# The last MLP of a two-layer decoder trunk in two phases: its first product by seven block products, the hidden layer through DRAM, then its second product

## The chip, the cores and the metric

The kernel runs on one core of a Trainium2 chip. The metric is the device time of one execution in microseconds. The kernel before was run three times: 2396.58, 2397.88 and 2399.75 us, median 2397.88 us. TensorE is called PE below, VectorE DVE, ScalarE ACT, GpSimd POOL and SyncE SP, as in the profile. "MM" is one matmul instruction.

## The reference, cut to what matters

Two decoder layers over 1024 tokens of width 1024, all in float32. Layer 0 mixes tokens with an mLSTM, layer 1 with latent attention on a shared K/V. After each mixer stands an MLP with a hidden width of 4096. The change touches the MLP of layer 1 alone, and of that only the second half of the tokens.

```python
D_MODEL, SEQ, DEPTH, D_FF = 1024, 1024, 2, 4 * 1024

def sqrelu_mlp(h, w1, w2):
    return jnp.square(jax.nn.relu(h @ w1)) @ w2

for l in range(DEPTH):
    ...                                            # mixer: y
    x = x + g1[:, None, :] * rmsnorm(y, norm_g[l, 1])
    h = modulate(rmsnorm(x, norm_g[l, 2]), sh2, sc2)
    y = sqrelu_mlp(h, mlp_w1[l], mlp_w2[l])
    x = x + g2[:, None, :] * rmsnorm(y, norm_g[l, 3])
```

## The kernel before, in words

**Numbers.** Each float32 product is made of three PE products. Both operands are split into a high part (the value rounded to the PE's fp32r format) and a low part (the rest). `mm3` (L230 to L233) issues low times high, high times low, high times high into one PSUM tile. The high part of a weight tile is an ACT cast (L189), the low part a DVE subtraction (L190); both are in `wsplit`.

**Tokens.** They are worked in two halves of 512. `hfs[0]` and `hfs[1]` hold what belongs to a half. Normalized activations lie with the model width on the partitions and 512 tokens along the row.

**The MLP** (`mlp`) has two kinds of steps. A hidden step (L947) takes 128 columns of the first matrix, makes 8 x 3 = 24 MMs of 128x512 into a `ps` tile, and then ReLU (L957), square (L958) and the split into `hd` (L470, L471). An up step (`up_rows`, L973) multiplies four hidden blocks by a 512-column block of the second matrix, 24 MMs of 128x512 into a `pm` tile, and a DVE addition (L198) sums the result into `y`. For the last half the call is `mlp(1, hfs[1], u1, [4] * 8, True)`: four hidden steps, then hidden and up steps alternate, and at the end up steps alone. Hidden values never leave SBUF.

**Buffers.** PSUM: `ps` has 2 buffers of one bank, `pc` 2 of one bank, `pm` 2 of two banks. SBUF: `k4` 24 tiles of 128x1024, `hd` 8, `ws` 8 (the split weights), `raw` 4 (where weights land by DMA), `tmc` 6 and `tmp` 3 of 128x512.

**Order.** The program is written as generators. `go` takes one step of the dense stream (the MLP) and ties what is issued to the last PE instruction so far, so PE runs in the order of the code. A scheduler orders the other engines by priority; what stands in a `high_priority` block comes earlier. Each engine then runs its list in order, and SP issues the DMAs in order. Before the last MLP `two_streams` runs the MLP of half 0 beside the mixer of half 1 (`mixer1`), whose last part, `post`, makes the normalized input of the last MLP.

**The fill.** Beside the last MLP runs the generator `all_out`, advanced by one after each of its steps: `x_to_rows(0)` (16 advances; eight sets of four PE transposes, L1572, ACT copies and DMAs), `along_rows` (L1586 to L1590), `rows_out` of half 0 (L1593 on: for each of four row tiles two ACT squares with a sum, L1606, whose result goes unread into a `ps` tile, then DVE work L1611 to L1616 and the output DMA), and `x_to_rows(1)`. `rows_out` of half 1 comes after the last MM.

Of the kernel before, what the change touches and what calls it, by code (L numbers as in the profile page):

```python
# [17 lines left out]
P = 128  # L18
# [64 lines left out]
def kernel(  # L83
# [39 lines left out]
    def k4v(dt=F32, b=512):  # L123
        return k4(dt)[:, :1024].rearrange("p (a b) -> p a b", b=b)
# [7 lines left out]
    def raw(dt=F32):  # L132
        return sb.tile([P, 1024], dt, tag="raw", bufs=RAW, name=f"raw_{next(uid)}")
# [13 lines left out]
    def ps():  # L147
        return pp.tile([P, 512], F32, tag="ps", bufs=2, name=f"ps_{next(uid)}")
# [10 lines left out]
    def scratch(shape, name):  # L159
        return dr.tile(shape, F32, tag=name, bufs=1, name=name)  # L160
# [21 lines left out]
    def paced():  # L182

        return tc.issue_after(pace[0]) if pace[0] else nullcontext()

    def wsplit(r, n):
        hi = sb.tile([P, 1024], F32R, tag="ws", bufs=WS, name=f"wh_{next(uid)}")
        lo = sb.tile([P, 1024], F32R, tag="ws", bufs=WS, name=f"wl_{next(uid)}")
        nc.scalar.copy(hi[:, :n], r[:, :n])  # L189
        i = nc.vector.tensor_sub(lo[:, :n], r[:, :n], hi[:, :n].bitcast(F32))  # L190
        if follow[0]:
            pace[0] = i.ins
        return hi, lo
# [31 lines left out]
    def wcols(w, c0, n=P, k0=0, nk=KD):  # L225
        return w[k0 * P : (k0 + nk) * P, c0 : c0 + n].rearrange("(k p) n -> p k n", p=P)

    pe_last = [None]

    def mm3(o, lh, ll, rh, rl, start, stop):  # L230
        nc.tensor.matmul(o, ll, rh, start=start, stop=False)  # L231
        nc.tensor.matmul(o, lh, rl, start=False, stop=False)  # L232
        pe_last[0] = nc.tensor.matmul(o, lh, rh, start=False, stop=stop)  # L233


    nc.scalar.preload_act_table_set("natural_log_exp_and_others")
# [239 lines left out]
    def normed(h, xs_, rstd, A, sh):  # L476

        for k in range(KD):
            with paced():
                nc.vector.scalar_tensor_tensor(  # L480
                    xs_[k], xs_[k], A[:, k : k + 1], rstd, ALU.mult, ALU.mult
                )
                split_mod(h.hi[k], h.lo[k], xs_[k], sh[:, k : k + 1])
            if k % 4 == 3:
                yield 1

    def along_tokens(dst, y):
# [450 lines left out]
    NF = DFF // P  # L938
    AHEAD = 2

    def mlp(l, hf, y, sizes, rows=False):


        w1, w2, h = mlp_w1[l], mlp_w2[l], hf.h2
        hids = {}

        def hidden(f):  # L947
# [24 lines left out]

        def up_rows(fs, i, last):  # L973


            G = len(fs)
            if G == 2:
                g, t0, t1 = i, 0, 4
            else:
                g, t0 = (i % 2, i // 2 * 2) if last else (i // 2, i % 2 * 2)  # L980
                t1 = t0 + 2
            key = (fs[0], g)
            final = last and G == 4 and i
# [12 lines left out]
            def block(pt, ws, t):  # L996
                for q, f in enumerate(fs):
                    w, (hh, hl) = ws[q // 2], hids[f]
                    mm3(
                        pt, hh[:, ts(t, P)], hl[:, ts(t, P)], w[0][:, q % 2], w[1][:, q % 2],  # L1000
                        q == 0, q == G - 1,
                    )

            def one(ws):


                for n, (t, h) in enumerate([(0, 1), (1, 1)] if i == 1 else [(i, 0), (i, 1)]):
                    if n:
                        yield "within"
                    pt = pc()  # L1010
                    block(pt, ws if i == 1 else ws[h], t)
                    accumulate((t, h), y.t[t][:, h], pt)

            def out(ws):
                for t in range(t0, t1):
                    if t % 2 == 0:
                        if t > t0:
                            yield "within"
                        b2 = pm()
                    block(b2[:, t % 2], ws, t)  # L1020
                    if t % 2:
                        for e in range(2):
                            accumulate((t - 1 + e, g), y.t[t - 1 + e][:, g], b2[:, e])

            return load, one if final else out

        def up_cols(fs, i, last):
            G = len(fs)
            n = KD // G

            def out(w):
# [12 lines left out]
            return lambda: wload([(0, 0, wcols(w2, i * n * P, n * P, fs[0], G))], n * P), out  # L1044

        up = up_rows if rows else up_cols
        steps, prev, f0 = [], [], 0
# [10 lines left out]
        ready = []  # L1058
        for n in range(len(steps) + AHEAD):
            if n < len(steps):  # L1060
                ready.append(steps[n][0]())
            if n >= AHEAD:
                yield from steps[n - AHEAD][1](ready.pop(0))

                yield steps[(n - AHEAD + 1) % len(steps)][1].__name__


    rope_d = scratch([2, P, S], "rope_d")
# [679 lines left out]
    A1 = gain(2, NG(0, 2), adac(0, SC2))  # L1748
    B1 = gate(3, NG(0, 3), adac(0, G2))

    def post(hf, y, B, src, A, sh):
# [5 lines left out]
        yield 0  # L1757
        hf.h2 = Split()
        yield from normed(hf.h2, y, rstd, A, sh)

# [126 lines left out]
    rope_perm()  # L1887


    z1 = FH(claim=True)  # L1890
    ya = [None, None]

    def mixer1(hf, z, attention):
        att = attention(hf)
        lat = latent(hf, lambda: next(att))
        next(lat)

        yield from to_x(hf, z)
        yield "fill"
        yield from lat  # L1900
        yield next(att)
        yield from att
# [6 lines left out]
        yield from post(hf, y, B2, x_cols, A3, adac(1, SH2))  # L1909
# [6 lines left out]
    u1 = FH(claim=True)  # L1916

    def all_out():
        yield from x_to_rows(0)
# [43 lines left out]
```

## Time and profile before

| what | value |
|---|---|
| median of three runs | 2397.88 us |
| span of the profiled execution | 2395.7 us |
| PE busy | 2364.8 us |
| DVE busy | 1550.3 us |
| ACT busy | 1054.9 us |
| moved by DMA | 374.48 MB, mean 156 GB/s |
| first hidden step of the last MLP | 2027.41 us |
| last MM starts | 2386.78 us |

All times of the trace count from the start of the span. The profiled execution's own time is its span, 2395.7 us; the median of the runs is 2.2 us above it. PE is busy for all but some 31 us of the span; a group's line gives busy time, the mean of one instruction in ns, and the idle time of the engine just before it. The start of an MM to the start of the next is its pace, and is shorter than its duration, because MMs are pipelined.

### The profile page before, as it was taken

How to read it: one execution, taken by the hardware profiler on the slowest of the kernel's cores; microseconds unless marked ns; L12 is line 12 of the kernel's file. 1: busy time of each engine (PE TensorE's matmuls, PEld its weight loads, DVE VectorE, ACT ScalarE, POOL GpSimd, SP SyncE). 2: the span in 40 equal slices, each digit the busy share in tenths (PEclk: the TensorE clock that was granted, in tenths of full speed). 3: DMA queues.
4: the chain of work that ended last, by engine and by line, in shares of the span. 5: the costliest groups of instructions: out<-in, count | busy, mean ns of one | idle time of the engine just before them, and what ended most of it. 6: DMA issues, size and time to landing. Idle time of an engine off the chain costs nothing.

```text
span 2395.7 us, 30518 instructions
## 1 busy us (share of the span) xinstructions
PE 2364.8 (99%) x11621; PEld 1945.5 (81%) x11621; DVE 1550.3 (65%) x2431; ACT 1054.9 (44%) x1712; POOL 18.3 (1%) x91
## 2 busy tenths in 40 slices
PE   7999999999999999999999999999999999999998
PEld 5888888788888887888888877888888888888886
DVE  6667866858656677877764867766566386353345
ACT  4355334655333454444444554344444353443333
POOL 1000000000000000000000000000000000000000
PEclk9999999999999999999999999999999999999999
DMA  8442654544654745545543444864424354354431
GB/s 310 148 143 81 192 178 134 165 132 150 189 171 152 243 138 179 159 160 186 168 137 114 153 162 153 260 240 133 139 97 150 105 167 128 101 189 140 144 99 62
DMA packets 377106, 374.48 MB, mean 156 GB/s; under 512 B 24355, under 2 KB 282464, under 8 KB 376960
## 3 DMA queue, kind: packets, MB, share of 16 engines
q1 hardware_dynamic: 376672, 372.44, 48.9%
q8 instruction: 91, 1.49, 0.3%
q14 instruction: 55, 0.45, 0.1%
q0 software_dynamic: 288, 0.10, 0.0%
HBM read 313.24 MB, written 59.24 MB: 155 GB/s over the span
## 4 chain that ended last, share of the span: by engine, by line
PE 91%; DVE 4%; DMA 3%; ACT 1%; issue 1%; SPq 0%; DVEq 0%; ACTq 0%
PE ps L231 17%; PE ps L232 17%; PE ps L233 17%; PE pm L231 10%; PE pm L232 10%; PE pm L233 10%; PE pc L1445 1%; PE pc L231 1%; PE pc L233 1%; PE pc L232 1%; PE pm L815 1%; PE pm L1331 1%; DMA raw<-in_mlp_w_dram 1%; DVE wl L190 1%; PE pm L1325 1%
## 5 line engine op out<-in xcount | busy, mean ns | idle before, releaser
L190 DVE TENSOR_TENSOR wl<-raw,wh 128x1024 fp32r<-128x1024 f32 (+2 forms) x366 | 438.7, 1202 | 449.5 <-ACT wh L189 442.3
L189 ACT CAST wh<-raw 128x1024 fp32r<-128x1024 f32 (+2 forms) x366 | 376.0, 1032 | 717.0 <-PE ps L231 392.2
L231 PE MATMUL ps<-k,wl 128*128 128x512 f32 x1528 | 611.0, 400 | 2.3 <-ACT k L671 1.4
L233 PE MATMUL ps<-k,wh 128*128 128x512 f32 x1528 | 601.0, 393 | 0.0
L232 PE MATMUL ps<-k,wh 128*128 128x512 f32 x1528 | 600.9, 393 | 0.0
L231 PEld LDWEIGHTS ps<-k,wl 128*128 128x128 f32 x1528 | 287.0, 188 | 69.7 <-issue 2.9
L233 PEld LDWEIGHTS ps<-k,wh 128*128 128x128 f32 x1528 | 287.0, 188 | 67.3 <-issue 0.5
L232 PEld LDWEIGHTS ps<-k,wh 128*128 128x128 f32 x1528 | 287.5, 188 | 63.6 <-issue 1.7
L198 DVE TENSOR_TENSOR k<-k,pm 128x512 f32<-128x512 f32 (+1 forms) x254 | 210.9, 859 | 107.0 <-PE pm L233 106.5
L231 PE MATMUL pm<-hd,wl 128*128 128x512 f32 x512 | 202.0, 394 | 0.4 <-ACT hd L470 0.4
L233 PE MATMUL pm<-hd,wh 128*128 128x512 f32 x512 | 199.8, 391 | 0.0
L232 PE MATMUL pm<-hd,wh 128*128 128x512 f32 x512 | 199.5, 390 | 0.2 <-DVE hd L471 0.2
L231 PE MATMUL pm<-wh,hd 128*128 128x512 f32 x488 | 192.9, 395 | 3.2 <-ACT raw L1337 2.9
L232 PE MATMUL pm<-wl,hd 128*128 128x512 f32 x488 | 191.3, 392 | 0.0
L233 PE MATMUL pm<-wh,hd 128*128 128x512 f32 x488 | 190.3, 390 | 0.0
L360 DVE SCALAR_TENSOR_TENSOR tma<-raw,cond,tma 128x512 f32<-128x512 f32 x168 | 125.6, 747 | 20.6 <-DMA raw<-in_kv_ada_w_dram 14.6
L471 DVE TENSOR_TENSOR hd<-tmp,hd 128x512 fp32r<-128x512 f32 x128 | 88.3, 690 | 56.8 <-ACT hd L470 56.5
L1337 ACT ACTIVATE raw<-pm,sm 128x128 f32<-128x128 f32 (+3 forms) x64 | 47.5, 742 | 151.3 <-DVE sm L1336 122.7
L232 PEld LDWEIGHTS pm<-hd,wh 128*128 128x128 f32 x512 | 96.2, 188 | 21.3 <-DVE hd L471 0.5
L231 PEld LDWEIGHTS pm<-hd,wl 128*128 128x128 f32 x512 | 96.1, 188 | 21.2 <-ACT hd L470 0.8
L233 PEld LDWEIGHTS pm<-hd,wh 128*128 128x128 f32 x512 | 96.1, 188 | 21.1
L231 PEld LDWEIGHTS pm<-wh,hd 128*128 128x128 f32 x488 | 91.6, 188 | 24.9 <-ACT raw L1337 5.5
(347 smaller groups left out, 3414.5 us busy)
## 6 DMA issues: line engine op xcount, KB each, us to landing
raw<-in_mlp_w_dram SPq DMA_DIRECT2D x256, 512.0 KB, 4.1
raw<-in_ada_w_dram SPq DMA_DIRECT2D x80, 512.0 KB, 4.3
raw<-in_a_w_in_dram SPq DMA_DIRECT2D x48, 512.0 KB, 4.1
xs<-k SPq DMA_DIRECT2D x40, 256.0 KB, 4.8
raw<-in_kv_ada_w_dram SPq DMA_DIRECT2D x16, 512.0 KB, 3.8
raw<-in_a_w_out_dram SPq DMA_DIRECT2D x16, 512.0 KB, 4.6
kd<-k SPq DMA_DIRECT2D x32, 256.0 KB, 3.7
vd<-k SPq DMA_DIRECT2D x32, 256.0 KB, 5.0
```

What stands on the lines that cost most here:

```text
L189: nc.scalar.copy(hi[:, :n], r[:, :n])
L190: i = nc.vector.tensor_sub(lo[:, :n], r[:, :n], hi[:, :n].bitcast(F32))
L198: return f(*a, **k)
L231: nc.tensor.matmul(o, ll, rh, start=start, stop=False)
L232: nc.tensor.matmul(o, lh, rl, start=False, stop=False)
L233: pe_last[0] = nc.tensor.matmul(o, lh, rh, start=False, stop=stop)
L360: nc.vector.scalar_tensor_tensor(acc, r[:, kk], cond[:, k : k + 1], acc, ALU.mult, ALU.add)
L471: nc.vector.tensor_sub(lo, u, hi.bitcast(F32))
L815: nc.tensor.matmul(nv[:, r, i], hf.PT[p_][:, r, cs], v[:, 2 * p_ + r], start=g == 0, stop=True,)
L1325: nc.tensor.matmul(o[:, :w], ql, kh, start=True, stop=False)
L1331: nc.tensor.matmul(o[:, :w], qh, kh, start=False, stop=True)
L1337: nc.scalar.activation(pr[:, :n], f, AF.Exp, bias=m, scale=SCALE, accum_out=l)
```

## The change

The last MLP is split in two phases.

**Its input.** `post` gets a `kept` generator for half 1. Instead of splitting the normalized activations as they are, it keeps them in float32, cuts them into four blocks (upper and lower half of the model width by first and second 256 tokens) and makes seven combinations of the blocks, each split into high and low (14 `k4` tiles). This stands at the end of `mixer1`.

**Phase one** (`seven`) takes pairs of 128 columns of the first matrix, 16 pairs. A pair is a 2 x 2 block matrix of weights (two halves of the model width by two column blocks). `load` fetches both columns (two DMAs of 512 KB), makes the weight combinations and splits them: three `wsplit` and one half-size split, which fill seven `ws` tiles, and four DVE sums of 128x512; all four `raw` tiles are in use at once. `product` multiplies one weight combination by one token combination: 4 x 3 = 12 MMs of 128x256. There are seven per pair where the direct way has eight. Products 1, 6, 5 and 3 are summed one after the other in one `ps` bank, products 7 and 4 in one bank of a `pm` tile, product 2 has the other bank. Between these sums ACT copies of 128x256 (products 1, 6, 7) and DVE additions (2, 5, 4) take the partial results out: a running sum is read and then added to further. After product 3 follow ReLU of the last quarter on ACT, a DVE maximum and an ACT square over the pair's 128x1024 tile, and a 512 KB DMA into the DRAM tensor `hidd`. The seven products of a pair are interleaved with those of the pair before: 1, (5), 2, (4), 6, (3), 7, those in brackets being of the pair before. The fill is advanced after every fourth product.

**Phase two** is `mlp` with `stored=True`: no hidden steps, and the 32 up steps alone. `fetch` reads a pair's hidden values back (512 KB into `raw`) and splits them into two `k4` tiles. The condition on `i` in `both` is evaluated when a step is loaded, after the loop over `i` has ended, so that `i` is 3 in each call. `fetch` is thus called for all `f` below 32, and with the two calls ahead of the loop there are 32 reads of `hidd` against 16 writes.

`up_front` and `both_halves` are new and not called.

```diff
-    def mm3(o, lh, ll, rh, rl, start, stop):
+    def mm3(o, lh, ll, rh, rl, start, stop, more=False):
...
+    def normed_kept(y, rstd, A, sh, parts):
...
+    def seven(l, pairs, B, out):
+        w1 = mlp_w1[l]
+        def load(p_):
+            with tc.high_priority(PRIO):
+                r1, r2 = raw(), raw()
+                for r, f in ((r1, 2 * p_), (r2, 2 * p_ + 1)):
+                    nc.sync.dma_start(r.rearrange("p (a b) -> p a b", b=P), wcols(w1, f * P))
+                lo_, hi_ = slice(0, 512), slice(512, 1024)
+                A = wsplit(r1, 1024)
+                t1, t2 = raw(), raw()
+                nc.vector.tensor_add(t2[:, lo_], r2[:, lo_], r2[:, hi_])
+                nc.vector.tensor_sub(t1[:, hi_], t2[:, lo_], r1[:, lo_])
+                nc.vector.tensor_sub(t1[:, lo_], r1[:, lo_], r2[:, lo_])
+                nc.vector.tensor_sub(t2[:, hi_], r1[:, hi_], t1[:, hi_])
+                T1 = wsplit(t1, 1024)
+                a22 = sb.tile([P, 1024], F32R, tag="ws", bufs=WS, name=f"wa_{next(uid)}")
+                T2 = wsplit(t2, 1024)
+                nc.scalar.copy(a22[:, lo_], r2[:, hi_])
+                nc.vector.tensor_sub(a22[:, hi_], r2[:, hi_], a22[:, lo_].bitcast(F32))
...
+        def product(u, i):
+            o = {1: u.b, 6: u.b, 5: u.b, 3: u.b, 2: u.x, 7: u.z, 4: u.z}[i]
+            (wh, wl), (bh, bl) = u.w[i], B[i]
+            for k in range(4):
+                mm3(o, wh[:, k], wl[:, k], bh[k], bl[k], i in (1, 2, 7) and k == 0, k == 3, more=i not in (1, 2, 7))
...
+            for u, i in ((cur, 1), (prev, 5), (cur, 2), (prev, 4), (cur, 6), (prev, 3), (cur, 7)):
+                if u:
+                    product(u, i)
+                    yield "hid"
...
+        def fetch(f):
+            with tc.high_priority(PRIO):
+                r, hi, lo = raw(), k4v(F32R), k4v(F32R)
+                nc.sync.dma_start(r, hidd[hf.i, f // 2])
+                split_wide(hi, lo, r.rearrange("p (a b) -> p a b", b=512))
...
+                    def both(load=load, f=4 * g + 2 * i):
+                        w = load()
+                        if i >= 2 and f < NF:
+                            fetch(f)
+                        return w
...
-    dense = mlp(1, hfs[1], u1, [4] * 8, True)
+    dense, n = seven(1, range(NF // 2), blocks1, one_half(hfs[1])), 0
+    while go(dense) is not end:
+        n += 1
+        if n % 4 == 0:
+            v = next(fill)
+    u1 = FH()
+    dense = mlp(1, hfs[1], u1, [], True, True)
```

**The order on PE.** Before, in the middle of the last MLP, an up step (tile `pm`) ends and a hidden step (tile `ps`) begins; the set of transposes between them is a step of the fill:

```order
9901 L232 MATMUL pm_17828<-wl_17751,hd_17708 128x512
9902 L233 MATMUL pm_17828<-wh_17750,hd_17708 128x512
9903 L1572 MATMUL pc_17855<-ident,tmc_17825 128x128 [waits DMAHW3_49,PE_49]
9904 L1572 MATMUL pc_17855<-ident,tmc_17825 128x128 x3
9905 L231 MATMUL ps_17869<-k_2966_16817,wl_17791 128x512 [waits DVE_49]
9906 L232 MATMUL ps_17869<-k_2967_16818,wh_17790 128x512 [waits Activation_49]
9907 L233 MATMUL ps_17869<-k_2966_16817,wh_17790 128x512
```

Now, in phase one, the end of a pair's product 7 (`pm_18491`) and the beginning of the next pair's product 1 (`ps_18622`):

```order
10369 L232 MATMUL pm_18491<-k_2996_17010,wl_18372 128x256
10370 L233 MATMUL pm_18491<-k_2997_17011,wh_18371 128x256
10371 L234 MATMUL pm_18491<-k_2996_17010,wh_18371 128x256
10372 L232 MATMUL ps_18622<-k_2977_16907,wl_18497 128x256 [waits DVE_49,Activation_49]
10373 L233 MATMUL ps_18622<-k_2978_16908,wh_18496 128x256
10374 L234 MATMUL ps_18622<-k_2977_16907,wh_18496 128x256
```

Each group of 24 MMs of 128x512 has become groups of 12 MMs of 128x256, and the first of them waits for the next pair's first split weights (`wl_18497`) and for a `ps` buffer.

**The order on ACT** around `rows_out` of half 0. Before, the squares (L1606) stand behind a hidden step's ReLU, square and split (L957, L958, L470):

```order
1423 L957 ACTIVATE tmp_17980<-ps_17955 128x512 [waits PE_49]
1424 L958 ACTIVATE tmp_17980<-tmp_17980 128x512 [waits Activation_49]
1425 L470 CAST hd_17954<-tmp_17980 128x512 [waits Activation_49]
1426 L1590 COPY k_3160_17985<-pc_17987 128x512 [waits PE_49]
1427 L1606 ACTIVATE ps_18075,sm_18074<-k_2071_11970 128x512
1428 L1606 ACTIVATE ps_18077,sm_18074<-k_2071_11970 128x512 [waits Activation_49]
1429 L1606 ACTIVATE ps_18137,sm_18136<-k_2072_11971 128x512 [waits Activation_49]
```

Now (the line is L1827) four squares stand between the last reading of a pair's `ps` tile (L1050, ReLU after product 3) and the partial sum of product 1 two pairs on (L1035), among the copy of product 7 (L1044), the square over the pair (L1079) and the casts of split weights (L189):

```order
1485 L1050 ACTIVATE hd_18705<-ps_18622 128x256 [waits PE_49]
1486 L1827 ACTIVATE ps_18827,sm_18826<-k_2071_11971 128x512 [waits Activation_49]
1487 L189 CAST wh_18788<-raw_18782 128x1024 [waits DVE_49]
1488 L1827 ACTIVATE ps_18829,sm_18826<-k_2071_11971 128x512 [waits Activation_49]
1489 L1044 COPY tmc_18941<-pm_18773 128x256 [waits PE_49]
1490 L1827 ACTIVATE ps_18907,sm_18906<-k_2072_11972 128x512 [waits Activation_49]
1491 L1079 ACTIVATE hd_18705<-hd_18705 128x1024 [waits DVE_49]
1492 L1827 ACTIVATE ps_18909,sm_18906<-k_2072_11972 128x512 [waits Activation_49]
1493 L189 CAST wh_18793<-raw_18783 128x1024 [waits DVE_49]
```

The four squares take, one after the other, the `ps` buffer that `ps_18622` has left, while the pair in work still holds the other one; the next pair's product 1 comes after them in that buffer.

More of the change, by code (lines that the diff above doesn't have):

```diff
@@ L484, in normed, with split_wide @@
             if k % 4 == 3:
+                yield 1
+    def split_wide(hi, lo, u):
+        nc.scalar.copy(hi, u)
+        nc.vector.tensor_sub(lo, u, hi.bitcast(F32))
+    def normed_kept(y, rstd, A, sh, parts):
+        for b in range(4):
+            with paced():
+                for k in (2 * b, 2 * b + 1):
+                    nc.vector.scalar_tensor_tensor(
+                        y[k], y[k], A[:, k : k + 1], rstd, ALU.mult, ALU.mult
+                    )
+                    nc.scalar.activation(y[k], y[k], AF.Identity, bias=sh[:, k : k + 1])
+                if parts[b]:
+                    split_wide(*parts[b], y.t[b])
+            if b % 2:
                 yield 1
@@ L939, with ahead_of, up_front, hidden @@
     AHEAD = 2
-    def mlp(l, hf, y, sizes, rows=False):
+    hidd = scratch([2, NF // 2, P, 2 * H], "hidd")
+    def ahead_of(steps):
+        ready = []
+        for n in range(len(steps) + AHEAD):
+            if n < len(steps):
+                ready.append(steps[n][0]())
+            if n >= AHEAD:
+                yield from steps[n - AHEAD][1](ready.pop(0))
+                yield steps[(n - AHEAD + 1) % len(steps)][1].__name__
+    def up_front(l, hf, pairs):
+        w1, h = mlp_w1[l], hf.h2
+        at = {}
+        def hidden(f):
+            def hid(w):
+                pt = ps()
+                for k in range(KD):
+                    if k == KD // 2:
+                        yield "within"
+                    mm3(pt, w[0][:, k], w[1][:, k], h.hi[k], h.lo[k], k == 0, k == KD - 1)
+                if f % 2 == 0:
+                    at[0] = k4v()
+                s = at[0][:, f % 2]
+                with tc.high_priority(PRIO):
+                    nc.scalar.activation(s, pt, AF.Relu)
+                    nc.scalar.activation(s, s, AF.Square)
+                    if f % 2:
+                        nc.sync.dma_start(hidd[hf.i, f // 2], at[0].rearrange("p a b -> p (a b)"))
+            return lambda: wload([(0, 0, wcols(w1, f * P))], P), hid
+        yield from ahead_of([hidden(f) for p_ in pairs for f in (2 * p_, 2 * p_ + 1)])
@@ L944, in mlp @@
+    def mlp(l, hf, y, sizes, rows=False, stored=False):
         w1, w2, h = mlp_w1[l], mlp_w2[l], hf.h2
         hids = {}
+        def fetch(f):
+            with tc.high_priority(PRIO):
+                r, hi, lo = raw(), k4v(F32R), k4v(F32R)
+                nc.sync.dma_start(r, hidd[hf.i, f // 2])
+                split_wide(hi, lo, r.rearrange("p (a b) -> p a b", b=512))
+            for e in range(2):
+                hids[f + e] = (hi[:, e], lo[:, e])
         def hidden(f):
@@ L1046, in mlp @@
         up = up_rows if rows else up_cols
+        if stored:
+            fetch(0)
+            fetch(2)
+            steps = []
+            for g in range(NF // 4):
+                for i in range(4):
+                    load, run = up(list(range(4 * g, 4 * g + 4)), i, g == NF // 4 - 1)
+                    def both(load=load, f=4 * g + 2 * i):
[3 more added lines that the diff above has]
+                        return w
+                    steps.append((both, run))
+            n = 0
+            for v in ahead_of(steps):
+                n += v != "within"
+                yield v if v == "within" else ("hid", "out")[n % 2]
+            return
         steps, prev, f0 = [], [], 0
@@ L1057, in mlp @@
         steps += [up(prev, i, True) for i in range(len(prev))]
[L1058 to L1065, printed above, removed]
+        yield from ahead_of(steps)
     rope_d = scratch([2, P, S], "rope_d")
@@ L1757, in post @@
         yield 0
+        if kept:
+            yield from kept(y, rstd)
+            return
         hf.h2 = Split()
@@ L1887 @@
     rope_perm()
+    blocks1 = {}
     z1 = FH(claim=True)
@@ L1908, in mixer1 @@
         yield 1
-        yield from post(hf, y, B2, x_cols, A3, adac(1, SH2))
+        yield from post(
+            hf, y, B2, x_cols, A3, adac(1, SH2), quarters(blocks1) if hf.i else None
+        )
     two_streams(mlp(0, hfs[1], z1, [2] * 14 + [4]), mixer1(hfs[0], z0, attention_first), bg_rest())
```

105 lines of the change are left out of this document (100 added, 5 removed).

## The prediction

> **What bounds the kernel now.** I read the page first: its busy shares, then the chain that ended last.
>
> ```profile
> span 2395.7 us, 30518 instructions
> PE 2364.8 (99%) x11621; PEld 1945.5 (81%) x11621; DVE 1550.3 (65%) x2431; ACT 1054.9 (44%) x1712; POOL 18.3 (1%) x91
> PE 91%; DVE 4%; DMA 3%; ACT 1%; issue 1%; SPq 0%; DVEq 0%; ACTq 0%
> ```
>
> PE is busy for 2364.8 of 2395.7 us and carries 91% of the chain, so the time falls only where PE has less to do, and rises wherever PE has to wait. Next the windows over the last MLP (PE, PE loads, DVE, ACT, POOL, then clock, DMA share and GB/s):
>
> ```profile
> 2000.00:2100.00 100.00, 100.00 (x444) 81.53 (x443) 38.55 (x44) 41.19 (x60) 0.00 (x0) 1.00 0.36 112
> 2100.00:2200.00 100.00, 100.00 (x446) 81.31 (x445) 52.12 (x88) 43.93 (x76) 0.00 (x0) 1.00 0.51 165
> 2200.00:2300.00 100.00, 100.00 (x446) 81.92 (x445) 37.77 (x43) 37.62 (x50) 0.00 (x0) 1.00 0.42 132
> ```
>
> Here PE never waits, while DVE and ACT are idle for half the time or more. That slack is what the change spends.
>
> **What the change saves on PE.** The paces come from starts in the timeline: a hidden step of 24 MMs of 128x512, and a run of 12 MMs of 128x256 elsewhere in the trace.
>
> ```profile
> 2061.05 0.39 PE L231 MATMUL ps<-k,wl 128*128 128x512 f32 x1
> ...
> 2066.60 0.39 PE L231 MATMUL pm<-wh,hd 128*128 128x512 f32 x1
> ```
>
> ```profile
> 1848.30 0.28 PE L231 MATMUL ps<-hd,k 128*128 128x256 f32 x1
> ...
> 1849.71 0.39 PE L231 MATMUL ps<-k,wl 128*128 128x512 f32 x1
> ```
>
> The wide step takes 5.55 us, 0.2312 each; the narrow run takes 1.41 us, 0.1175 each. Before, the hidden steps have 32 x 24 = 768 wide MMs, 177.6 us. Now there are 16 x 7 x 12 = 1344 narrow ones, 157.9 us. The saving is 19.7 us; 0.001 us of doubt in the narrow pace is 1.3 us. I take 19.5. The up steps keep their 768 MMs.
>
> Each MM has its own weight load:
>
> ```profile
> L231 PEld LDWEIGHTS ps<-k,wl 128*128 128x128 f32 x1528 | 287.0, 188 | 69.7 <-issue 2.9
> ```
>
> A load takes 188 ns, more than the narrow pace, yet the narrow run above changes its weights with every MM and still paces at 117.5 ns. If loads were the limit, 1344 x 0.188 = 252.7 us would stand against 177.6, 75 us slower. [...] I give it under 1 in 100.
>
> **What phase one asks of DVE and of the landings.** Durations by form, and three starts that show DVE's pace:
>
> ```profile
> L190 DVE TENSOR_TENSOR wl<-raw,wh 128x1024 fp32r<-128x1024 f32 x350 | 426.6, 1222 | 444.5 <-ACT wh L189 440.1 <-PE ps L233 2.9 <-DMA lw<-wl 0.9
> L471 DVE TENSOR_TENSOR k<-k,k 128x512 fp32r<-128x512 f32 x26 | 16.9, 684 | 0.0
> L661 DVE COPY k<-ps 128x256 f32<-128x256 f32 x16 | 6.7, 420 | 5.1 <-PE ps L233 5.1
> L1339 DVE TENSOR_SCALAR raw<-raw,sm 128x1024 f32<-128x1024 f32 x8 | 6.0, 754 | 0.6
> ```
>
> ```profile
> 1959.32 0.68 DVE L198 TENSOR_TENSOR k<-k,pm 128x512 f32<-128x512 f32 x1
> 1959.92 1.22 DVE L190 TENSOR_TENSOR wl<-raw,wh 128x1024 fp32r<-128x1024 f32 x1
> 1961.05 0.68 DVE L463 TENSOR_SCALAR tmc<-pc 128x512 f32<-128x512 f32 x1
> ```
>
> Back to back, a 512 sum costs 0.60 and a 1024 subtraction 1.13, some 0.09 less than the duration. A pair needs three low parts of 1024, five operations of 512, three additions of 256 and one maximum of 1024: by durations 3.67 + 3.42 + 1.26 + 0.75 = 9.1 us, by pace some 8.1. A pair on PE is 84 x 0.1175 = 9.87 us. So DVE is no bound by itself, but it has gone from four tenths to eight or nine, and waits no longer vanish.
>
> The loop that matters runs through the `raw` tiles. All four are taken by a pair, and the second column of the next pair can be fetched only when the subtraction for T1 has read its tile.
>
> ```profile
> raw<-in_mlp_w_dram SPq DMA_DIRECT2D x256, 512.0 KB, 4.1
> k<-xr SPq DMA_DIRECT2D x8, 512.0 KB, 6.6
> ```
>
> From A's low part over one 512 sum, the maximum and T1's low part: 1.13 + 0.60 + 0.67 + 1.22 = 3.6 us. Then the column lands, 4.1 us, or up to 5 when another 512 KB travels beside it (an estimate between these two rows). Then three sums of 512 and one addition of 256 (0.33 by pace) stand before the next A: 2.1 us. The period is 9.8 to 10.7 us, against 9.87 on PE. In most pairs the fill adds a set of four transposes:
>
> ```profile
> 1975.99 0.39 PE L231 MATMUL pm<-wh,hd 128*128 128x512 f32 x1
> 1976.21 0.40 PE L232 MATMUL pm<-wl,hd 128*128 128x512 f32 x1
> 1976.45 0.39 PE L233 MATMUL pm<-wh,hd 128*128 128x512 f32 x1
> 1976.68 0.38 PE L1572 MATMUL pc<-ident,tmc 128*128 128x128 f32 x2
> 1976.82 0.48 PE L231 MATMUL pm<-wh,hd 128*128 128x512 f32 x1
> 1977.13 0.39 PE L232 MATMUL pm<-wl,hd 128*128 128x512 f32 x1
> 1977.36 0.40 PE L233 MATMUL pm<-wh,hd 128*128 128x512 f32 x1
> ```
>
> The two transposes recorded put 0.22 us between MMs that otherwise start every 0.23 us (1.37 for five paces of 0.23), so a set is 0.2 to 0.4, a cost of before too; with it PE's pair takes about 10.2 and the loop mostly hides. I charge 3 us over 16 pairs, 1 to 8 as ends (0.06 to 0.5 a pair).
>
> **Where I expect the gain to go: `rows_out` of half 0.** Its squares write to `ps` tiles, and in phase one `ps` holds running sums.
>
> ```profile
> L1606 ACT ACTIVATE ps<-k 128x512 f32<-128x512 f32 x16 | 9.6, 598 | 14.8 <-DVE k L198 13.3 <-DVE sm L1613 1.5
> L1606 ACT ACTIVATION_READ_ACCUMULATOR ps<-k 128x1 f32 x16 | 3.0, 187 | 0.0
> L663 ACT COPY k<-ps 128x256 f32<-128x256 f32 x16 | 6.0, 372 | 30.2 <-PE ps L233 30.1
> L189 ACT CAST wh<-raw 128x1024 fp32r<-128x1024 f32 x350 | 365.3, 1048 | 708.4 <-PE ps L231 391.8 <-DMA raw<-in_mlp_w_dram 101.4 <-PE pm L231 80.4
> ```
>
> A square and its sum take 0.598 + 0.187 = 0.79 us. Before, they found a free `ps` buffer, as the windows show PE at 100.00 there. In the order of after, four squares use the buffer that product 3 leaves, and the next pair's product 1 must wait for the fourth. In between stand the ReLU (0.37), a cast (1.05), the copy of product 7 (0.37) and the square over the pair (1024, priced as the cast, 1.05): 4 x 0.79 + 2.84 = 6.0 us. PE has only product 7 to do, 1.41, so it waits 4.6 us; with the latencies about 4.9. The next two row tiles have no cast and no big square before the fourth square: 3.16 + 0.74 - 1.41 = 2.5, with latencies 2.9. Behind this wait DVE finds its additions late: the addition of product 4 queues behind the two products of 512 and the small operations of `rows_out`, and the low parts of the next A come after it. I read 1.25 and 1.85 us more of PE waiting from the durations above. Together 4.9 + 2.9 + 3.1 = 10.9, less a little that the loop above wins back: 10.5 us. If the squares slide into ACT's idle time, 4; if DVE's backlog runs through a further pair, 14.
>
> A long wait may also cost clock. Early in the trace there is one:
>
> ```profile
> 28.03 0.80 PE L231 MATMUL pm<-k,wl 128*128 128x512 f32 x1 [4.36 <-ACT k L473]
> ```
>
> ```profile
> 25.00:30.00 5.00, 1.97 (x5) 0.48 (x5) 4.96 (x9) 2.74 (x5) 0.00 (x0) 0.50 1.05 387
> 30.00:35.00 5.00, 5.00 (x19) 3.61 (x18) 4.96 (x7) 0.76 (x1) 0.00 (x0) 0.86 1.05 385
> ```
>
> After 4.36 us without work the MM took 0.80 instead of 0.39, and the granted clock was 0.50, back to 0.86 on average in the next window, where full clock came after some 1.4 us (0.14 of 5 us is 0.7 lost, at half clock 1.4 long). From 28.03 to 31.4 at half clock half of 3.4 us, 1.7, is lost. I charge 1.6 for the first wait, 0 for the second. [...]
>
> **Start and turn.** The seven combinations add 14 casts and 14 subtractions of 512 and eight sums of 512 at the end of `mixer1`, less eight operations of 512 on DVE that go. That is some 14 x 0.684 = 9.6 us more on DVE. It lies beside up and hidden steps of half 0 that stand in front of the first product in PE's order; I charge 0.5, ends 0 and 2. If that cover were gone, the 9.6 would show.
>
> At the turn from phase one to phase two the first up step needs hidden tiles that were read twice, and the later read is the one it uses. That read needs a `raw` tile which the last pair's a22 subtraction frees, so landing (4.1), cast (1.05) and subtraction (1.22) lie behind it: 6.4 us, of which the last products cover some 4. I charge 2.5, ends 1 and 5. After that, an up step of 5.5 us asks DVE for two low parts (weights and hidden values) and sums of about 1.3 us: under 4 us, and DMA for 1 MB, 190 GB/s where the early windows show 385. The double reading is hidden. Without up steps to cover it, it would cost its 16 extra landings and splits.
>
> The end, `rows_out` of half 1 after the last MM, is as before.
>
> **The sum.** -19.5 + 3 + 10.5 + 1.6 + 2.5 + 0.5 = -1.4 us on the profiled 2395.7, so 2394.3 for such an execution. The median of the runs stands 2.2 above the span: 2397.88 - 1.4 = 2396.5 us. About 0.2%, 4.8 us, is what a measurement of this kernel can tell from no change.
>
> **The rivals.**
>
> *The waits are short (faster).* The squares fall into gaps of ACT and landings stay at 4.1: stall 4, loop 1, clock 0, turn 1.5, start 0.5, together 7. The time is 2397.88 - 12.5 = 2385.4; between it and my sum lie 2386 to 2393. For it: ACT is idle over half of these windows, and the scheduler may place squares earlier than the order of their durations suggests. Against it: in the order of after the next product 1 stands behind the fourth square in each case.
>
> *The `raw` loop becomes the bound (slower).* The store of 512 KB and the other column travel with the second column, and it takes longer than the 4.1 of the row. The point from which this decides is a landing above 4.5 us, where the period passes PE's 10.2. At 5.2, the period is 10.9, and 16 x 0.7 = 11 us replace the 3: sum +6.6, 2404.5. At the 6.6 of the other row, 16 x 2.1 = 34 us, 2427. For it: all `raw` tiles in use, DVE at nine tenths. Against it: the mean traffic, 1.5 MB in 10 us, is 150 GB/s, as in the windows of before.
>
> *The change doesn't do what it says.* The double reading makes phase two late instead of hidden, for example by `raw` tiles that are taken: 32 steps x 0.2 us = 6 us more, 2403. DVE's 4 us of 5.5 speak against it.
>
> **How the numbers follow.** My forecast, the gain eaten within 0.2%: 0.40. Short waits: 0.28. The loop: 0.24. Phase two late: 0.08. So faster 0.28, same 0.40, slower 0.32. The range takes the faster case to its 2386 and the loop up to a landing of 5.5 us (period 11.2, 16 us for the 3: 2409.5): 2386 to 2409. The forecast's own range is 2393 to 2402.
>
> **What would show it.** PE's idle before `ps` MMs in phase one, with ACT's squares as releaser, near 10 us: right; under 5: the first rival. A distance between the pairs' first products of 9.9 to 10.4 us away from the squares: right; 10.9 or more with `raw` landings above 5 us: the second. PE waiting in every up step of phase two: the third. I am wrong if PE in phase one doesn't pace at 0.1175, or if PE's waits stand at another place than the squares and the turn.

## The result, and the profile after

The changed kernel takes 2414.89 us, the median of four runs (2409.03 to 2417.83), against 2398.82 us for the kernel before in the same sessions. The ratio is 1.0062, with a 95% interval of 1.0046 to 1.0078: slower by about 15 us, where no measurable change was forecast, and outside the range. The profiled execution has a span of 2411.6 us and a time of 2413.4 us.

The page of after, in the rows that answer to those of before:

```profile
span 2411.6 us, 32160 instructions
PE 2360.6 (98%) x12197; PEld 1968.3 (82%) x12197; DVE 1666.6 (69%) x2605; ACT 1100.8 (46%) x1774; POOL 17.9 (1%) x87
PE 81%; DMA 8%; DVE 7%; ACT 2%; issue 2%; SPq 0%; DVEq 0%; ACTq 0%
```

PE's busy time fell by only 4 us while the span grew by 16. More telling is the chain: DMA went from 3% to 8%, DVE from 4% to 7%. Transfers now stand in the path.

The windows of after, cut at the first product, before and behind `rows_out` of half 0, at the turn, and at the last MM (us, then PE, PE loads, DVE, ACT, POOL, the granted clock, DMA share, GB/s):

```profile
2027.90:2046.00 18.10, 17.57 (x146) 17.16 (x145) 13.83 (x20) 9.77 (x16) 0.00 (x0) 1.00 0.29 88
2046.00:2152.00 106.00, 98.91 (x793) 95.81 (x792) 76.89 (x118) 58.94 (x91) 0.00 (x0) 0.98 0.60 190
2152.00:2208.00 56.00, 46.88 (x353) 45.64 (x353) 46.08 (x85) 31.60 (x62) 0.00 (x0) 0.91 0.51 164
2208.00:2222.50 14.50, 13.03 (x108) 12.62 (x107) 10.39 (x15) 9.92 (x16) 0.00 (x0) 1.00 0.98 336
2222.50:2402.40 179.90, 179.80 (x788) 146.12 (x788) 113.18 (x141) 74.12 (x93) 0.00 (x0) 1.00 0.61 205
```

Before, the same work is one stretch in which PE never waits:

```profile
2027.40:2387.00 359.60, 359.60 (x1589) 293.43 (x1587) 154.65 (x220) 143.60 (x223) 0.00 (x0) 1.00 0.38 121
```

The last MLP takes 374.5 us against 359.6. Phase two runs without a stop, 179.9 us. Phase one takes 194.6, where its 1344 MMs at 0.1175 need 157.9. Of the 36.7 between them, 18.2 are PE idle (0.5 + 7.1 + 9.1 + 1.5), and 5.4 are lost to a lower clock, as worked out below. The rest, some 13, is PE at work: the fill's transposes (a set of four at 2077.43 takes 0.60 us) and row matmuls, and the slow first MMs after the stops (0.20 and 0.22 us to the next start at 2080.11 and 2179.46, against 0.12). In before, fill and the like are 4.5 us of the whole stretch (359.6 less 1536 MMs at 0.2312).

What PE waits for in the second of these windows and in the third:

```profile
PE ps L232 <- DVE wl L190: 4.9, 5, 2.1
PE ps L232 <- ACT hd L1050: 1.3, 1, 1.3
PE pc L1793 <- DMA tmc<-xs: 0.8, 3, 0.3
```

```profile
PE ps L232 <- ACT ps L1827: 6.0, 2, 3.8
PE ps L232 <- DVE wl L190: 1.8, 2, 1.3
PE pc L1793 <- DMA tmc<-xs: 1.3, 2, 1.1
```

The third window shows the squares of `rows_out` (L1827 in after) where they were forecast. The second was forecast nearly free of waits. There PE waits for the low part of a split weight. DVE in turn waits at L1011, the first sum that reads the second column (from 2050 to 2150):

```profile
DVE raw L1011 <- DMA raw<-in_mlp_w_dram: 12.0, 9, 2.7
```

The chain of waits for that stretch leads back from DVE to the same transfer:

```profile
2046.35 6.07 DMA raw<-in_mlp_w_dram
...
2054.65 1.22 DVE wl L190
2055.97 0.42 issue
2056.39 1.22 DVE wl L190
2057.64 6.14 DMA raw<-in_mlp_w_dram
...
2068.44 1.15 DVE wl L190
2069.60 7.24 DMA raw<-in_mlp_w_dram
2077.00 0.55 issue
```

This is the `raw` loop of the prediction, turn by turn: T1's low part ends, the second column is asked for, it lands 6.07, 6.14 and 7.24 us later, the sums and low parts follow, and T1's low part ends again. From 2046.35 to 2057.64 a turn takes 11.3 us, to 2069.60 it takes 12.0. The sum had 4.1 us for the landing, or 5 at most. Over the ten fetches between 2045 and 2152 the second column lands in 5.3 to 7.2 us, 6.0 on average, and the first, where its landing is on record, in 4.0 to 4.7. The order on SP shows who travels beside it:

```profile
2056.50 1.86 SPq L1007 DMA_DIRECT2D raw<-in_mlp_w_dram  x2
2058.41 0.58 SPq L1789 DMA_DIRECT2D tmc<-xs  x1
2059.35 0.48 SPq L1080 DMA_DIRECT2D hidd<-hd  x1
```

Both columns of a pair, a row block of the fill and the store of the hidden values are asked for within 3 us. The columns and the store each start as an instruction ends that they wait for, two of DVE at 2056.47 and 2057.61 and one of ACT at 2059.32, and these ends lie together at this place of the turn.

### The profile page after: what moved, and what is told of

It reads as the page before. It is cut to its first block, busy times and chain, and to the rows that moved or that the text cites. A ratio compares the mean times of both kernels' runs of the same rounds, so it can differ in the third digit from the quotient of the medians.

```text
span 2411.6 us, 32160 instructions
## 1 busy us (share of the span) xinstructions
PE 2360.6 (98%) x12197; PEld 1968.3 (82%) x12197; DVE 1666.6 (69%) x2605; ACT 1100.8 (46%) x1774; POOL 17.9 (1%) x87
## 4 chain that ended last, share of the span: by engine, by line
PE 81%; DMA 8%; DVE 7%; ACT 2%; issue 2%; SPq 0%; DVEq 0%; ACTq 0%
PE ps L232 14%; PE ps L233 14%; PE ps L234 14%; PE pm L232 9%; PE pm L233 9%; PE pm L234 9%; DMA raw<-in_mlp_w_dram 4%; DVE wl L190 2%; PE pc L1666 1%; PE pc L232 1%; DVE tma L361 1%; PE pc L234 1%; PE pc L233 1%; ACT wh L189 1%; PE pm L1552 1%
## 5 line engine op out<-in xcount | busy, mean ns | idle before, releaser
L190 DVE TENSOR_TENSOR wl<-raw,wh 128x1024 fp32r<-128x1024 f32 (+2 forms) x382 | 458.1, 1202 | 324.3 <-ACT wh L189 306.0
L189 ACT CAST wh<-raw 128x1024 fp32r<-128x1024 f32 (+2 forms) x382 | 392.7, 1032 | 598.8 <-PE ps L232 245.2
L232 PE MATMUL ps<-k,wl 128*128 128x512 f32 (+1 forms) x1528 | 585.0, 383 | 16.3 <-DVE wl L190 7.4
L233 PE MATMUL ps<-k,wh 128*128 128x512 f32 (+1 forms) x1528 | 575.4, 377 | 0.0
L234 PE MATMUL ps<-k,wh 128*128 128x512 f32 (+1 forms) x1528 | 574.9, 376 | 0.0
L232 PEld LDWEIGHTS ps<-k,wl 128*128 128x128 f32 x1528 | 289.7, 190 | 75.9 <-ACT wh L189 7.4
L232 PE MATMUL pm<-hd,wl 128*128 128x512 f32 x512 | 202.0, 394 | 0.4 <-ACT hd L471 0.4
L232 PEld LDWEIGHTS pm<-hd,wl 128*128 128x128 f32 x512 | 96.1, 188 | 21.1 <-ACT hd L471 0.8
L232 PE MATMUL pm<-wh,hd 128*128 128x512 f32 x256 | 101.9, 398 | 2.6 <-ACT raw L1558 2.3
L234 PE MATMUL pm<-wh,hd 128*128 128x512 f32 x256 | 100.0, 391 | 0.0
L233 PE MATMUL pm<-wl,hd 128*128 128x512 f32 x256 | 99.9, 390 | 0.0
L232 PE MATMUL pm<-wh,k 128*128 128x512 f32 x232 | 92.0, 397 | 1.5 <-DVE k L490 1.5
L1165 ACT ACTIVATE tmp<-ps 128x512 f32<-128x512 f32 x96 | 56.9, 593 | 79.0 <-PE ps L234 78.9
```

The lines of the kernel that those rows point to most:

```text
L232: nc.tensor.matmul(o, ll, rh, start=start, stop=False, **m)
L233: nc.tensor.matmul(o, lh, rl, start=False, stop=False, **m)
```

## The experiments

Theory L: the second column's landing, some 6 us instead of 4 to 5, sets the pair's period through the `raw` buffers. Its rival D: DVE, with 9.1 us of work a pair and its waits for buffers, sets it whatever lands when. Theory Q: the squares in `ps` cost some 10 us beside that. Times are medians, each with its ratio to the kernel before on the same chip; pairs are the distances of the ACT copies after product 1 (L1035 of after), which in after are 11.6 us on average over the ten pairs ahead of `rows_out`. The ratio of after is itself known to 0.16% either way and those of the runs below to some 0.13%, so a difference from after of under 5 us cannot be told from none by the medians; the traces say then where time moved.

**The combined weights in other buffers.**

```diff
-                t1, t2 = raw(), raw()
+                t1, t2 = hd(), hd()
```

> The edit: the two combined weight tiles of a pair take hd buffers, which stand empty in phase one, so that the four raw buffers hold the columns of two pairs and the next pair's columns can be fetched without waiting for a subtraction. Theory L (the changed kernel's pairs take 11.6 us because the second column's landing of 6 to 7 us stands in a loop with the subtractions through the raw buffers): the distance of the pairs' first products falls from 11.6 to between 10.0 and 10.5 us, some 14 us over ten pairs, and the time from 2414.9 to between 2397 and 2403 us. Rival D (VectorE itself, 9.1 us of work a pair with its waits for free split-weight buffers, sets the period): the distance stays above 11 us and the time above 2410.

Measured: 2405.79 us, ratio 1.0028 (1.0017 to 1.0040). The same ten pairs take 10.8 us on average, a little over the 10.5 expected. The window that had 793 MMs now has 860, at full clock, and PE's waits in it fall to the two rows below:

```profile
2046.00:2152.00 106.00, 104.68 (x860) 102.37 (x859) 82.76 (x129) 62.58 (x96) 0.00 (x0) 1.00 0.62 199
```

```profile
PE pc L1810 <- DVE tmc L1807: 0.8, 1, 0.8
PE ps L232 <- DVE wl L190: 0.4, 1, 0.4
```

DVE does the same work per pair and more of it in this window (82.76 us against 76.89), so D falls: PE stops waiting when the fetch stops waiting, though DVE itself still waits for the second column (16.9 us from 2050 to 2150). The time fell by 9, not by the 14 expected. The squares took part of it back: the two pairs around `rows_out` now take 17.6 and 18.5 us against 19.0 and 14.7 before the edit, PE waits 9.4 us for the squares by the list of waits over the whole phase, and at each of these two stops the granted clock fell to 0.50 for 6.8 us.

**The squares away from PSUM.**

```diff
-                junk = ps()
+                junk = tmp()
```

> The edit: the unread result of the row squares goes to an SBUF tile in place of a ps buffer of PSUM. Theory Q (the two pairs around the output rows of half 0 lose 10 us because the next product 1 waits for the fourth square's buffer): the waits of TensorE for these squares, 12.4 us in all in the trace, go, the two pairs take 24 us rather than 33.7, and the time falls by 8 to 11 us to between 2404 and 2407. Rival (the weights' loop would have made these pairs late anyhow, since VectorE has the rows' work too): the time falls by under 4 us.

Measured: 2412.20 us, ratio 1.0056 (1.0043 to 1.0068), 2.7 us below after, which the medians cannot tell from no gain. The waits for the squares are gone and the two pairs take 11.2 and 10.9, so Q is right about what makes them late. (PE's waits for the squares were 6.0 us in after; the 12.4 of the expectation adds the 6.4 of the weight loads, which stand at the same two stops.) But over the whole phase PE waits elsewhere:

```profile
PE ps L232 <- DVE wl L190: 8.5, 12, 1.4
PE pc L1793 <- DMA tmc<-xs: 6.3, 4, 3.2
```

In after these two rows were 6.7 and 2.1. The two pairs gain 11.6 us, and most of it goes elsewhere in the phase: the next two pairs take 26.4 us against 22.2 in after, where behind the long stops DVE did not wait for the second column in the first of them (L1011 at 2187.96), and from the last pair's copy to the first up step it takes 19.7 against 14.3, with a wait of 3.2 for a row block and 3.4 us at half clock with it. Phase one falls from 194.6 to 192.0 only. The expected 8 to 11 is missed: with one stop gone, others came in its place.

**One reading back of each hidden pair.**

```diff
-                    def both(load=load, f=4 * g + 2 * i):
+                    def both(load=load, f=4 * g + 2 * i, i=i):
```

> The edit: the loop variable is bound when a step is made, so that each pair of hidden blocks is read back once: 16 reads of 512 KB rather than 32. If the double reading is hidden behind the up steps but for the turn between the phases: 1 to 3 us faster, 2412 to 2414. If it makes the up steps late: the distance of phase two from first to last matmul falls from 179.7 to 176 us or less and the time by 4 to 6 us more.

Measured: 2410.49 us, ratio 1.0048 (1.0036 to 1.0061), 4.4 us below after by the medians and 1.8 by the profiled spans. Phase two takes 179.9 us as in after, so the 16 extra readings are hidden there. What the profile gains lies ahead of it, where phase one went from 194.6 to 192.1: the wait of 1.5 us for a split of the hidden values (L490) before the first up step is gone.

**The three edits together.**

> The three edits together. If the losses are separate, they add: 14 + 9 + 2 = 25 us faster than the changed kernel, 2390 us, 0.4% faster than the kernel before. If VectorE is the next bound behind the weights' loop, pairs stay at 11 us or more and the time at 2400 or above, no faster than before.

Measured: 2396.51 us, ratio 0.9988 (0.9979 to 0.9997). It is 18.4 us below after, about the three gains by themselves, 16.2, and less than the 25 expected. The ten pairs take 10.9 us on average and the two around `rows_out` 12.6 and 12.2. Phase one takes 176.7 us at full clock:

```profile
2031.30:2208.00 176.70, 169.60 (x1394) 165.97 (x1393) 142.33 (x230) 106.22 (x176) 0.00 (x0) 1.00 0.63 201
```

**Two phases with the wide products of before** (the combinations and seven products replaced by `up_front`, which the change brings but doesn't call).

```diff
-    dense, n = seven(1, range(NF // 2), blocks1, one_half(hfs[1])), 0
-    while go(dense) is not end:
-        n += 1
-        if n % 4 == 0:
-            v = next(fill)
+    dense = up_front(1, hfs[1], range(NF // 2))
+    while (d := go(dense)) is not end:
+        if d != "within":
+            v = next(fill)
```

> The edit: phase one made of the wide hidden steps of before (768 matmuls of 128x512, no combinations, no seven products), stored to DRAM and read back as in the changed kernel; phase two as changed. It prices the two phases alone. If they cost only the turn and what of the fill no longer finds a place: the last MLP takes 177.6 + 6 + 180 = 364 us against 359.5 before, 2401 to 2404 us. If the way through DRAM were what costs the changed kernel its 16 us: 2410 us or more.

Measured: 2404.37 us, ratio 1.0021 (1.0012 to 1.0030). So the two phases and the way through DRAM together cost some 5 us without the seven products, and not 16; the run does not part the one from the other. Its phase one has no wait, its phase two 2.1 us of waits and a short stretch at a lower clock:

```profile
2026.70:2210.00 183.30, 183.30 (x808) 148.12 (x807) 58.55 (x81) 82.24 (x132) 0.00 (x0) 1.00 0.59 181
2210.00:2393.30 183.30, 181.24 (x782) 146.51 (x781) 111.95 (x140) 72.98 (x92) 0.00 (x0) 0.99 0.57 194
```

**The fill after every seventh product.**

```diff
-        if n % 4 == 0:
+        if n % 7 == 0:
             v = next(fill)
```

> The edit: the fill is advanced after every seventh product rather than every fourth, so that the output rows of half 0 with their squares and row sums fall into phase two, and fewer transposes and row transfers into phase one. Theory L with Q: the pairs still take 11.0 to 11.6 us, since the raw loop stands, but none takes 14 to 19; phase one falls from 194.6 to between 180 and 187 us, the time to between 2402 and 2408. Rival (the row transfers of the fill are what lengthens the landing): pairs at 10.3 or less, phase one under 175, the time under 2398.

Measured: 2411.28 us, ratio 1.0046 (1.0032 to 1.0059). The ten pairs take 11.7 us on average, none of the others over 11.8, and PE waits 16.0 us in phase one for low parts of weights (L190). Four row blocks were asked for between 2046 and 2152 where after has seven, and the pairs are no shorter, so the row transfers of the fill have little part in the long turn. Phase one fell by 7.7 us to 187.0, but phase two, which now has `rows_out`, rose by 5.4 to 185.3, so the expected time was missed.

**Without the stores.** Only the first pair's hidden values are stored, and each `fetch` reads that one, so 15 stores are left out and phase two works on the first pair's values alone.

```diff
-                nc.sync.dma_start(hidd[hf.i, p_], s.rearrange("p a b -> p (a b)"))
+                if p_ == 0:
+                    nc.sync.dma_start(hidd[hf.i, p_], s.rearrange("p a b -> p (a b)"))
...
-                nc.sync.dma_start(r, hidd[hf.i, f // 2])
+                nc.sync.dma_start(r, hidd[hf.i, 0])
```

> The edit: only the first pair's hidden values are stored, and each reading back takes that one; the 15 other stores of 512 KB are left out. If the store is what lengthens the second column's landing, this landing falls from 6 to 7 us to 5 or less and the pairs from 11.6 to 10.6 or less, phase one by 10 us, the time to 2405 or less. If the two columns lengthen each other and the store has little part: pairs at 11.2 or more, the time at 2411 or more.

Measured: 2409.31 us, ratio 1.0039 (1.0026 to 1.0053). The pairs take 11.3 us on average, 0.3 less than in after, or 5 us over 16 pairs; the time fell by 5.6. Both are near what can be told from none: if the store has a part, it is the smaller one.

**Without the first column.** The first column is fetched once and copied by ACT for each pair, so 15 pairs work with the first pair's column in place of their own.

```diff
-        w1 = mlp_w1[l]
+        w1, kept_ = mlp_w1[l], hd()
...
-                for r, f in ((r1, 2 * p_), (r2, 2 * p_ + 1)):
-                    nc.sync.dma_start(r.rearrange("p (a b) -> p a b", b=P), wcols(w1, f * P))
+                for r, f in ((kept_, 2 * p_), (r2, 2 * p_ + 1)):
+                    if r is r2 or p_ == 0:
+                        nc.sync.dma_start(r.rearrange("p (a b) -> p a b", b=P), wcols(w1, f * P))
+                nc.scalar.copy(r1, kept_)
```

> The edit: the first column of each pair is not fetched (but for the first pair's, which ScalarE copies into the raw buffer for every pair), so that the second column's transfer has no other column beside it; 15 transfers of 512 KB are left out, the raw buffers and all waits for them stay. If the two columns, asked for 1.1 us apart, lengthen each other's landing: the second column lands in 4.0 to 4.8 us rather than 6 to 7, the pairs take 10.0 to 10.6 us, and the time is 2400 to 2404 us. If the landing is long for another cause (the store, the row transfers, the issue itself): landing above 5.5, pairs above 11, the time above 2408.

Measured: 2401.99 us, ratio 1.0012 (1.0002 to 1.0022), 12.9 us below after. All `raw` buffers and their waits are as in after; what changed is the landing (the first column's own landing falls away too, but DVE's waits at L1011 in after were for the second). The first row is after's, for both columns from 2046 to 2152, the second that of this kernel, for the second column alone:

```profile
DMA to landing us min/median/max: 4.0/5.5/7.2
```

```profile
DMA to landing us min/median/max: 4.1/4.4/5.4
```

DVE's waits for the second column are gone from the list. The ten pairs take 10.6 us, and PE waits for nothing in that window:

```profile
2046.00:2152.00 106.00, 105.98 (x876) 104.20 (x876) 85.50 (x131) 73.71 (x110) 0.00 (x0) 1.00 0.48 157
```

So it is the pair's other column, asked for 1.1 to 1.7 us ahead, that makes most of the landing's excess, and the landing that makes the pair long.

**A further version**: the combined weights in `hd` buffers, one reading back, and the fill after every seventh product.

> The edits: combined weight tiles in hd buffers, one reading back of each pair, and the fill after every seventh product. No long wait is left in phase one: pairs at 10.2 to 10.6 us, phase one 166 to 170 us against 176.7 with the three edits of the run before this, phase two 180, the time 2388 to 2391 us, 0.4% below the kernel before. If VectorE's backlog rather than the named waits were left, phase one stays above 174 and the time above 2394.

Measured: 2395.12 us, ratio 0.9977 (0.9966 to 0.9987), some 4 us below the kernel before by the medians and 5.5 by the ratio. Phase one takes 170.8 us with pairs of 10.2 to 11.0 but for the last, 12.3, phase two 183.2:

```profile
2030.20:2201.00 170.80, 167.48 (x1377) 164.27 (x1376) 129.65 (x195) 100.58 (x157) 0.00 (x0) 1.00 0.55 174
2201.00:2384.20 183.20, 183.20 (x805) 148.16 (x805) 107.76 (x162) 65.02 (x103) 0.00 (x0) 1.00 0.55 186
```

Phase one stands just above what was expected; the time is above it by 4 us, as the fill that left phase one is paid in phase two.

## Why the prediction was wrong, point by point

**The saving on PE** was right as far as the pace goes; the 19.5 us by themselves no run isolates. Narrow MMs pace at 0.12 us in after where PE doesn't wait:

```profile
2080.42 0.28 PE L234 MATMUL ps<-k,wh 128*128 128x256 f32 x1
2080.54 0.28 PE L232 MATMUL ps<-k,wl 128*128 128x256 f32 x1
```

Against the wide products in the same two phases (183.3 us for phase one), the last version's phase one is 12.5 us shorter, with some 3 us of PE idle left in it and fewer steps of the fill. What was too low is PE's own pair with its fill, 10.2 us: without the first column, where PE never waits, it is 10.6. The rival with weight loads as the limit did not come: the pace is 0.12 us with loads of 188 ns (median of L232 in after).

**The step that failed** is the charge for the `raw` loop: "I charge 3 us over 16 pairs, 1 to 8 as ends". The mechanism, the buffers and the point from which it decides ("a landing above 4.5 us") were right, and stood as the second rival with a chance of 0.24; the size was off. By the prediction's own sign, a distance of 10.9 or more with landings above 5 us, it is this rival that came. The loop was priced with a landing of 4.1 from a row of the kernel before, where columns are asked for some 5 us apart (11 in the 60 us from 2000), and with 5 as its end. In the changed kernel the two columns follow each other by 1.1 to 1.7 us, and the second lands in 5.3 to 7.2, 6.0 on average. By the rival's own formula, 3.6 + 6.0 + 2.1 = 11.7 us, near the 11.6 measured. Over ten pairs that is 116.4 us, where 102 were forecast and 2 of the 3 charged: 12 us too much in that stretch alone. The run without the first column takes 105.9 for them, so 10.5 of the 14.4 above 102 go with the landing, and 3.9 are PE's own pair with its fill. The range ended at a landing of 5.5. The argument against the rival, that the mean traffic is no higher than before (190 GB/s against 165 in the busiest window shown), was no argument: a mean says nothing about two transfers asked for together.

**The squares** came out near their number, "10.5 us", partly by luck: the two pairs take 33.7 us against 2 x 11.6, so 10.4, but that holds 3.9 us lost at half clock, which the sum charges apart. PE's waits for the squares were 3.8 and 2.2 us where 4.9 and 2.9 were forecast, the 0.3 and 0.4 us of latencies in these being the author's estimate that no row shows (PE began 0.05 us after the readout of the fourth square, at both stops), and in place of the 3.1 for DVE's backlog two waits for DVE follow in later pairs, 1.8 us together. Their order on ACT is the forecast one. And they did not stand alone, as the second experiment shows.

**The clock** was charged with 1.6 us for the first stop and 0 for the second. The 0 is a term that no run shows: after the second stop, of 2.2 us, the clock was 0.50 for 3.4 us. In all the granted clock was 0.50 in three stretches:

```profile
2081.20:2084.60 3.40, 3.40 (x18) 3.40 (x18) 1.11 (x1) 1.67 (x3) 0.00 (x0) 0.50 0.70 194
2163.10:2169.90 6.80, 5.20 (x24) 5.20 (x25) 5.17 (x15) 3.20 (x8) 0.00 (x0) 0.50 0.84 273
2180.20:2183.60 3.40, 3.40 (x18) 3.40 (x18) 2.59 (x9) 2.75 (x7) 0.00 (x0) 0.50 0.48 174
```

PE was busy for 12.0 us in them. A narrow MM starts every 0.214 us there (2081.27 to 2084.48, 15 paces) and every 0.118 at full clock (2170.09 to 2172.81, 23 paces), so 5.4 of the 12.0 are lost. The first belongs to the loop and not to the squares, and the stops ahead of the first and the third, 2.1 and 2.2 us by the waits, were shorter than the 4.36 us of the row that the price was taken from.

**Start and turn.** The first product begins at 2027.88, 0.5 us later than the first hidden step of before, as charged. PE has 1.5 us idle in the last window of phase one, the charge was 2.5. Phase two is not late by the double reading, as forecast. What the sum has no term for is the rest of the split in two phases: with wide products it costs 5 us, of which 2.1 are PE's waits and some 1.5 are lost in 3.4 us at half clock in phase two, an estimate from the paces above, and neither of these is in after's phase two.

**Together**: the last MLP takes 14.9 us more than before in the profiled execution, where the sum has 1.4 less, so 16.3 are to be explained. The ten pairs make 12 of them, above all the loop. Squares and clock around `rows_out`, charged with 12.1, make 13.3 above two pairs of 10.2, so they explain about 1. The rest, some 3, lies in the later pairs and the fill and is not parted further. Nor is it settled how much of the 1.5 us lost at half clock in the ten pairs is the loop's and how much the clock's, since the half clock there follows a stop that the loop made.

## What to carry to other kernels

The landing of the same 512 KB went with what was asked for beside it, 6.0 us on average behind the pair's other column and 4.4 (median) without it: before a change puts a transfer into a loop, list what else is asked for in the same 3 us, and price the landing with all of it. If a buffer couples the fetch of the next piece to the end of the work on this one, give the intermediate tiles other buffers first; here two names in one line were worth 9 us, more than the squares, whose stop of 3.8 us was the longest in the list of waits. And a gain on the bounding engine must be checked against the slack of the others after the change: PE had 20 us less to do, and the change spent the cover that DVE and the transfers had lived on.

## What the runs showed of the hardware

The granted clock fell to 0.50 after stops shorter than the 4.36 us of the prediction's row. In after, PE stood from the end of four transposes at 2078.03 until 2080.11, the wait shown in brackets, and the 3.4 us ahead of the half clock were not all idle: PE was busy in 1.32 of them.

```profile
2077.43 0.60 PE L1793 MATMUL pc<-ident,tmc 128*128 128x128 f32 x4
2080.11 0.35 PE L232 MATMUL ps<-k,wl 128*128 128x256 f32 x1 [2.08 <-DVE wl L190]
```

```profile
2077.80:2081.20 3.40, 1.32 (x12) 1.12 (x10) 3.40 (x6) 2.33 (x4) 0.00 (x0) 1.00 0.00 0
```

In the run with the fill after every seventh product a longer wait, 3.31 us, left the granted clock at 1.00. PE was busy in 1.80 and 1.69 us of the two stretches of 3.4 us that hold it:

```profile
2082.91 0.36 PE L232 MATMUL ps<-k,wl 128*128 128x256 f32 x1 [3.31 <-DVE wl L190]
2077.80:2081.20 3.40, 1.80 (x16) 1.59 (x14) 1.80 (x4) 0.39 (x1) 0.00 (x0) 1.00 0.24 74
2081.20:2084.60 3.40, 1.69 (x14) 1.72 (x15) 3.40 (x5) 2.46 (x4) 0.00 (x0) 1.00 0.01 5
2084.60:2088.00 3.40, 3.40 (x31) 3.40 (x30) 1.66 (x3) 1.68 (x3) 0.00 (x0) 1.00 0.89 259
```

In the run with the wide products a stop of only 1.82 us (3.40 less 1.58) was followed by half clock:

```profile
2256.50:2259.90 3.40, 1.58 (x7) 1.24 (x7) 3.40 (x5) 2.94 (x3) 0.00 (x0) 1.00 0.42 146
2259.90:2263.30 3.40, 3.40 (x9) 2.65 (x8) 3.02 (x4) 0.00 (x0) 0.00 (x0) 0.50 0.74 240
```

So the length of a stop alone does not decide: 3.31 us left the clock at 1.00, while 1.82 and 2.08 us stood ahead of 0.50. The half-speed stretches of after are 3.4, 6.8 and 3.4 us long. What decides is not shown here.
